# Conditioning rows kept in the heads' stage, decay rows by GpSimd's queue, and a head's tasks at fixed pieces

## The chip, the cores and the metric

The kernel runs on one core of a Trainium2 chip. A core has TensorE (PE, matmuls), VectorE (DVE), ScalarE (ACT), GpSimd (POOL) and SyncE (SP). Data come from the device's memory by DMA; SP, ACT and POOL each issue DMAs from their own instruction stream, in its order, so a DMA whose destination is not free holds up what stands behind it there. The metric is the device time of one execution in microseconds (us).

## The reference

Two layers over 256 latent and 256 context tokens of width 2048. Layer 0 is bidirectional retention with 8 heads (query and key width 256, value width 512), layer 1 windowed attention. Each layer is modulated by a projection of the conditioning vector ("ada"):

```python
c_act = silu(c); cc_act = silu(c_ctx)
mod_l = c_act @ ada_w[i] + ada_b[i]          # latent tokens; mod_c the same with cc_act
sh, sc, gt = split(mod, 3)
h = rms_norm(x, norm_gain[i]) * (1 + sc) + sh
# layer 0, per head: q, k (rope on the latent tokens), v, g = split(h @ w_in)
scores = (q @ k.T) * decay                   # gamma^(distance), one gamma for each direction and head
o = scores @ v
y = (rms_norm(o) * norm_gain * silu(g)) @ w_out
x = x + gt * y                               # and the same for the context tokens
```

## The kernel before

Numbers are fp32. An operand is split into a high part of a type that the PE takes (`wh`, `r_h`, made by ACT) and the rest (`wl`, `r_l`, made by DVE), and each product is three matmuls, L144 to L146 (`mm3`). The stages, in the order of time: up to about 137 us the inputs, layer 0's ada sums and the queries and keys of heads 0 and 1; to 235 us the q/k projections of heads 2 and 3; to 555 us the values; **555 to 1241 us the heads' stage**; to 1560 us the output projection, in a form with seven block products (M1 to M7) instead of eight, fed from `uB_d`; then the attention layer.

A **piece** is one load of 128x1024 weights (`load_w`: `wraw<-in_w` by SP, `wh` by ACT, `wl` by DVE) with the 24 matmuls that use it; `gemm_ws` runs eight pieces into four PSUM tiles `acc` and calls `hook` after each. In the heads' stage every head has a gate GEMM, and heads 4 to 7 a q/k GEMM ahead of it; heads 0 to 3 fetch q and k from DRAM (`qkr<-qk_d`). All raw blocks (weights, ada's blocks, the values) pass through one ring of five `wraw` tiles; there are three of `wh` and of `wl`.

What else is done for a head hangs on the hook, as **tasks**: `evac` (rope on q and k: ACT copies `sw`, DVE `t`, then the split), `v_load` (`wraw<-v_d` and its split), `decays` (the loads `rows<-gamT_d` and `dd<-skew_d`), `scores` (four; they read `rows` and `dd`), `output_tasks` (outputs, `ossq` sums of squares on POOL, `norm`, then `spill` and `parts`, which writes `ue` and `sg` to `uB_d`). Before, the tasks lie in one list, `pump` takes one or two of them after each piece, and what is left at a GEMM's end is run there. Beside them the hook calls `ada_step`: layer 1's and the gate's ada sums, 224 DVE instructions in all (L678, `wraw<-wraw,crow` and `ajunk<-wraw,crow`), each a block of weights times a row `crow` that is the same in all partitions; and `sums`, which prepares sums of output weights in DRAM (`wS_d`: a plain copy by ACT's queue and an accumulating DMA by POOL's, behind a tiny copy `pin_t`).

The framework's scheduler sets each engine's order from the program; `tc.issue_after(i)` keeps an instruction behind `i`. `last_lo`, `last_hi` and `last_ev` name the latest `wl`, the latest `wh` and the end of the latest `evac`.

Of the kernel before, what the change touches and what calls it, by code (L numbers as in the profile page):

```python
# [22 lines left out]
T = 512  # L23
# [29 lines left out]
def backbone(ctx: ExitStack, tc, xT_d, w0_d, wo0_d, w1_d, wo1_d, adaS_d, adaB_d,  # L53
# [68 lines left out]

    last_lo, last_hi, last_wl, last_pe, last_ev = [None], [None], [None], [None], [None]

# [213 lines left out]
    crow_d = dram.tile([2, D], F32, name="crow_d")  # L338
    adap_cm = tc.tile_pool(name="adap", bufs=1, side="right")
    adap = adap_cm.__enter__()  # L340
    pb_cm = tc.tile_pool(name="pb", bufs=1, side="right")
# [319 lines left out]

    def ada_parts(where, parts, ntk):
        for layer, kind in parts:
            part = 3 * layer + kind - 2
            asum = const.tile([P, 2, KB, ntk], F32, name="asum", tag=f"asum{ntk}")
            for q in range(2):
                pool, tags = where()
                crow = [pool.tile([P, 1024], F32, name="crow", tag=g) for g in tags[:ntk]]
                for t in range(ntk):
                    nc.sync.dma_start(out=crow[t], in_=crow_d[t, q * 1024:(q + 1) * 1024].unsqueeze(0)  # L670
                                      .to_broadcast([P, 1024]))
                yield "row"
                for kb in range(KB):
                    raw = load_raw(adaB_d[16 * part + kb, q].rearrange("p (a c) -> p a c", a=2))
                    for t in range(ntk):
                        flat = raw.rearrange("p a c -> p (a c)")
                        junk = pool.tile([P, 1024], BF16, name="ajunk", tag="ajunk") if t < ntk - 1 else flat
                        nc.vector.scalar_tensor_tensor(  # L678
                            out=junk, in0=flat, scalar=1.0, in1=crow[t],
                            op0=ALU.mult, op1=ALU.mult, accum_out=asum[:, q, kb, t:t + 1])  # L680
# [8 lines left out]
    def crows():  # L689
        return adap, ("crow0", "crow1")  # L690

    jobs = chain(ada_parts(crows, ((0, 2), (1, 0), (1, 1)), 2), ada_parts(crows, ((1, 2),), 1))
    sums = sum_jobs()

    def behind():
        return tc.issue_after(last_ev[0]) if last_ev[0] is not None else ExitStack()

    def ada_step(n=1):
        for _ in range(n):
            with tc.issue_after(last_lo[0]), behind():  # L700
                next(jobs, None)

    def ada_rest():
        for _ in jobs:
            pass

    with tc.tile_pool(name="ph", bufs=1) as ph:
# [155 lines left out]
        for _, f in later:  # L863
            f()

    pb_cm = tc.tile_pool(name="pb", bufs=1, side="right")
    pb = pb_cm.__enter__()
# [66 lines left out]
    if True:  # L934
# [11 lines left out]

        def v_load(h, i):
            raw = load_raw(v_d[h, :, 2 * i:2 * i + 2])
            for t in range(2):
                with behind():  # L950
                    split(slot_h(4 + 2 * i + t)[:, :], slot_l(4 + 2 * i + t)[:, :], raw[:, t])

        state = {"n": 0}

        def qk_evac(ps, i, base):
# [9 lines left out]
            nc.vector.tensor_tensor(out=t1, in0=t1, in1=sw, op=ALU.add)  # L965
            return split(slot_h(sl)[:, 0:L], slot_l(sl)[:, 0:L], t1)

# [3 lines left out]
        def decays(h):  # L971
            rows = pb.tile([P, 512], F32, name="rows", tag="rows", bufs=2)
            for dr in range(2):
                src = gamT_d[dr, 0:2, h, :].unsqueeze(0).to_broadcast([P, 2, P])
                nc.scalar.dma_start(out=rows[:, 256 * dr:256 * dr + 256].rearrange("p (k t) -> p k t", k=2), in_=src)
            dd = pb.tile([P, P], F32, name="dd", tag="dd", bufs=2)
            nc.scalar.dma_start(out=dd, in_=skew_d[h, 127:127 + P * 254].rearrange("(p x) -> p x", x=254)[:, 0:P])
            return rows, dd

        def scores(h, base, kb, rows, dd):  # L980
            if True:
# [9 lines left out]
                if kb >= 2:  # L991
                    d2 = pb.tile([P, L], F32, name="d2", tag="d2", bufs=2)
                    nc.vector.tensor_scalar(out=d2, in0=rows[:, L:T], scalar1=gam[:, 6 + kb - 2, h:h + 1],
                                            scalar2=None, op0=ALU.mult)
                    nc.vector.scalar_tensor_tensor(out=d2, in0=rows[:, 0:L],
# [86 lines left out]
        def evac(h, get, ks):  # L1082
            for k in ks:
                last = qk_evac(get(k), k, 0)
                last_ev[0] = last.ins if h >= 4 else None

# [5 lines left out]

        def nothing():
            pass

        def hook():
            state["n"] += 1
            n = state["n"]
# [6 lines left out]
        rate, sg = [1], None  # L1105
        rd[0] = decays(0)
        qkr = fetch(0)
        for h in range(H):
            if h < 4:
                outs = output_tasks(h - 1, sg) if h else []  # L1110
                rate[0] = 2 if h else 1
                e = [lambda g=qkr, i=i: evac(h, g, (i, 2 + i)) for i in range(2)]
                v = [lambda i=i: v_load(h, i) for i in (1, 0)]
                sc = score_tasks(h)
                if h:
                    tasks.extend([e[0], outs[0], e[1], outs[1], nothing, v[0], v[1], outs[2], sc[0], sc[1],
                                  outs[3], outs[4], sc[2], sc[3]])
                else:
                    tasks.extend([nothing, nothing, lambda e=e: (e[0](), e[1]()), lambda v=v: (v[0](), v[1]()), nothing,
                                  lambda sc=sc: (sc[0](), sc[1]()), sc[2], sc[3]])  # L1120
            else:
                tasks.extend(output_tasks(h - 1, sg))
                tasks.insert(2, nothing)
                rate[0] = 1
                accs = gemm_ws(w0_d, 3 * h, 8, h_mov, T, hook=hook)
                while tasks:
                    pump()
                evac(h, lambda k: accs[k], range(4))
                if h == H - 1:
                    break  # L1130
                tasks.extend([lambda i=i: v_load(h, i) for i in (1, 0)] + score_tasks(h))
            if h < 3:
                qkr = fetch(h + 1)
            tasks.insert(2, lambda: rd.update({h + 1: decays(h + 1)}))
            accs = gemm_ws(w0_d, 3 * h + 2, 8, h_mov, T, hook=hook)
            while tasks:
                pump()
            sg = gates(h)
            for j in range(4):
                nc.scalar.activation(sg[j // 2][:, j % 2, :], accs[j], AF.Silu)  # L1140

        sg = gates(H - 1)
        outs = output_tasks(H - 1, sg, gated=False)
        plan = ([lambda: v_load(H - 1, 1), lambda: v_load(H - 1, 0)] + score_tasks(H - 1)[:1],
                score_tasks(H - 1)[1:], outs[:1], outs[1:2] + [(M1, 2), (M1, 3)],
                [(M1, 4), (M1, 5), (M1, 6), (M4, 0), (M4, 1)], outs[2:3] + [(M4, 5), (M4, 6), (M4, 2), (M4, 3)],
                outs[3:] + [(M4, 4), (M1, 0), (M1, 1)])
# [17 lines left out]

    ada_rest()
    pb_cm.__exit__(None, None, None)
# [3 lines left out]
    with tc.tile_pool(name="pc", bufs=1, side="right") as pc:  # L1171
# [507 lines left out]
```

## Time and profile before

| | |
|---|---|
| median of 3 runs | 1986.68 us (1985.29 to 1989.74) |
| profiled execution | 1988.66 us, of which the span, first to last instruction, is 1986.9 us |
| mean granted TensorE clock | 0.993 |
| busy share of the span: PE, DVE, ACT, POOL | 97%, 75%, 41%, 19% |
| DMA traffic | 476 MB, mean 240 GB/s |

A profile row names line, engine, operation and the tiles `out<-in`. "Idle before" is the time in which the engine stood still ahead of the instruction, and the name after the arrow is what it waited for. `SPq`, `ACTq` and `POOL ... DMA_DIRECT2D` are DMA issues. Matmul durations overlap: one takes 0.39 us, but one starts every 0.227 us in the rows of a stretch without a stall.

### The profile page before, as it was taken

The numbers are of one execution on the slowest core, as the hardware profiler recorded it, in microseconds if no ns is written. First come the engines' busy times: TensorE is split into PE (matmuls) and PEld (weight loads), VectorE is DVE, ScalarE is ACT, GpSimd is POOL, SyncE is SP. The second block draws the span as 40 slices with busy tenths as digits, with TensorE's granted clock in tenths as the row PEclk, the third lists the DMA queues.
The fourth block names the chain that finished last, engine by engine and source line by source line (L and its number), as shares of the span: only waits on it lengthen the run. The fifth ranks groups of instructions, "written<-read, shape, count | busy, mean of one in ns | idle before, by whom it ended". The sixth has DMA issues, their size and how long they took to land. (4 is left out here: it accounts for less than half of the span.)

```text
span 1986.9 us, 26032 instructions
## 1 busy us (share of the span) xinstructions
PE 1925.6 (97%) x9420; PEld 1581.1 (80%) x9420; DVE 1488.7 (75%) x2250; ACT 820.6 (41%) x1218; POOL 387.2 (19%) x415
## 2 busy tenths in 40 slices
PE   8999999999989999998999999999999999999999
PEld 4678878777778778876787788888888888888887
DVE  5567687887858898777887887877779745777764
ACT  4233334334334332232232234455555434766653
POOL 1203222222212444522324031100000010000001
PEclk9999999999999999999999999999999999999999
DMA  9969788889898878878897977677777324444364
GB/s 391 410 248 303 231 238 264 265 245 294 257 283 261 266 246 256 279 237 254 241 312 220 320 278 270 209 233 260 273 235 246 109 89 159 138 139 148 127 201 149
DMA packets 144378, 476.09 MB, mean 240 GB/s; under 512 B 17625, under 2 KB 38585, under 8 KB 138617
## 3 DMA queue, kind: packets, MB, share of 16 engines
q1 hardware_dynamic: 107232, 372.64, 54.2%
q0 software_dynamic: 13360, 43.79, 11.2%
q10 hardware_dynamic: 23656, 58.00, 8.7%
q8 instruction: 74, 1.21, 0.2%
q14 instruction: 56, 0.45, 0.1%
HBM read 443.37 MB, written 99.14 MB: 273 GB/s over the span
## 5 line engine op out<-in xcount | busy, mean ns | idle before, releaser
L114 DVE TENSOR_TENSOR wl<-wraw,wh 128x1024 fp32r<-128x1024 f32 x416 | 511.5, 1235 | 272.9 <-ACT wh L136 263.3
L136 ACT CAST wh<-wraw 128x1024 fp32r<-128x1024 f32 x415 | 434.6, 1052 | 676.6 <-DMA wraw<-in_w 203.2
L144 PE MATMUL acc<-hT_h,wh 128*128 128x512 f32 x928 | 366.0, 394 | 14.5 <-DVE t L963 8.2
L146 PE MATMUL acc<-hT_h,wl 128*128 128x512 f32 x928 | 361.7, 392 | 7.2 <-DVE wl L114 7.1
L145 PE MATMUL acc<-hl,wh 128*128 128x512 f32 x928 | 363.1, 391 | 0.0
L144 PEld LDWEIGHTS acc<-hT_h,wh 128*128 128x128 f32 x928 | 175.5, 189 | 55.3 <-issue 11.4
L146 PEld LDWEIGHTS acc<-hT_h,wl 128*128 128x128 f32 x928 | 175.1, 189 | 47.2 <-DVE wl L114 10.2
L326 POOL COPY pin_t<-wl 128x1 f32<-128x1 f32 x128 | 101.2, 790 | 548.5 <-DVE wl L114 540.6
L145 PEld LDWEIGHTS acc<-hl,wh 128*128 128x128 f32 x928 | 175.5, 189 | 34.9
L678 DVE SCALAR_TENSOR_TENSOR wraw<-wraw,crow 128x1024 f32<-128x1024 f32 x128 | 165.8, 1300 | 11.8 <-DMA crow<-crow_d 8.5
L245 POOL TENSOR_TENSOR rs<-ms,mhalf 128x4 f32<-128x4 f32 (+1 forms) x23 | 32.4, 1409 | 595.1 <-DVE ms L239 294.9
L678 DVE SCALAR_TENSOR_TENSOR ajunk<-wraw,crow 128x1024 bf16<-128x1024 f32 x96 | 127.4, 1327 | 13.9 <-DMA crow<-crow_d 9.8
L146 PE MATMUL acc<-wh,hl 128*128 128x512 f32 x320 | 125.0, 391 | 0.0
L328 POOL DMA_DIRECT2D wS_d<-in_wo x128 | 101.0, 791 | 8.9 <-issue 5.9
L136 ACT CAST wh<-vt 128x1024 fp32r<-128x1024 f32 x48 | 50.5, 1053 | 100.8 <-DVE vt L117 77.1
L114 DVE TENSOR_TENSOR wl<-vt,wh 128x1024 fp32r<-128x1024 f32 x48 | 58.8, 1224 | 40.1 <-ACT wh L136 39.5
L1044 POOL TENSOR_TENSOR ue<-sg 128x512 f32<-128x512 f32 x38 | 71.5, 1888 | 74.6 <-DVE sg L1034 30.9
L144 PE MATMUL pm<-r_h 128*128 128x512 f32 (+1 forms) x216 | 76.7, 355 | 7.3 <-DVE sg L1026 6.3
L145 PE MATMUL pm<-r_l,r_h 128*128 128x512 f32 (+1 forms) x216 | 76.0, 352 | 4.3 <-DVE r_l L114 4.3
L145 PE MATMUL acc<-wl,hT_h 128*128 128x512 f32 x192 | 75.6, 394 | 1.3 <-DVE wl L114 1.3
L144 PE MATMUL acc<-wh,hT_h 128*128 128x512 f32 x192 | 74.0, 392 | 1.6 <-ACT wh L136 1.6
L146 PE MATMUL pm<-r_h,r_l 128*128 128x512 f32 (+1 forms) x216 | 75.5, 350 | 0.0
(312 smaller groups left out, 3678.0 us busy)
## 6 DMA issues: line engine op xcount, KB each, us to landing
wraw<-in_w SPq DMA_DIRECT2D x288, 512.0 KB, 5.4
wraw<-in_adaB SPq DMA_DIRECT2D x128, 512.0 KB, 5.4
wraw<-in_wo SPq DMA_DIRECT2D x80, 512.0 KB, 4.2
wS_d<-in_wo ACTq DMA_DIRECT2D x128, 256.0 KB, 5.2
wS_d<-in_wo POOLq DMA_DIRECT2D x128, 256.0 KB, 6.4
wraw<-wS_d SPq DMA_DIRECT2D x64, 512.0 KB, 4.8
araw<-in_adaS SPq DMA_DIRECT2D x28, 1024.0 KB, 11.9
wraw<-uB_d SPq DMA_DIRECT2D x20, 512.0 KB, 4.5
```

The source lines that it names most:

```text
L114: return nc.vector.tensor_tensor(out=out, in0=a, in1=hi.bitcast(F32), op=ALU.subtract)
L136: last_hi[0] = nc.scalar.copy(wh, raw).ins
L144: nc.tensor.matmul(ps, lhsT=ah, rhs=bh, start=start, stop=False, skip_group_check=skip)
L145: nc.tensor.matmul(ps, lhsT=ah, rhs=bl, start=False, stop=False, skip_group_check=skip)
L146: return nc.tensor.matmul(ps, lhsT=al, rhs=bh, start=False, stop=stop, skip_group_check=skip).ins
L245: nc.gpsimd.tensor_tensor(out=rs, in0=ms, in1=mhalf.to_broadcast([P, n]), op=ALU.pow)
L326: pin = nc.gpsimd.tensor_copy(pin_t, last_wl[0][:, 0, 0:1].bitcast(F32)).ins
L328: nc.gpsimd.dma_start(out=wS_d[i, r, q, x], in_=wo0_d[(*SUMS[i][1], r, q, x)], accum_op=ALU.add, max_dma_last_dim=4096)
L678: nc.vector.scalar_tensor_tensor(out=junk, in0=flat, scalar=1.0, in1=crow[t], op0=ALU.mult, op1=ALU.mult, accum_out=asum[:, q, kb, t:t + 1])
L1044: (nc.vector if now else nc.gpsimd).tensor_tensor(out=ue, in0=x, in1=y, op=op)
```

## The change

1. The four `crow` rows (two tokens, two halves) are loaded once at the heads' stage's start by POOL's queue and stay (three tiles of a new pool `adapB`, one of the pool `top`); before, SP loaded a pair of rows again at each half of each part, 14 loads in all.
2. `rows` and `dd` are loaded by POOL's queue, not ACT's, into one tile each instead of two, and for the head itself instead of the next one.
3. The tasks of a head stand in a list by piece. `v_load` now only issues the loads; the splits are a task of their own, `v_split`, some pieces later and behind the current `wl` and `wh`. The first instruction of `d2` waits for the current `wl` too.
4. Ada steps: up to two more after some pieces of the q/k projections of heads 2 and 3, and fixed numbers per piece in the heads' stage.
5. `sums`: every third piece, from piece 33 on two of three, instead of three of four; the rest after single stages of the output projection.
6. The last head's `uB_d<-ue` stores go by POOL's queue instead of ACT's, its value load moves to its q/k GEMM, and the preparations of M1 start earlier in its last GEMM.

Instructions by engine as ordered: PE and DVE the same number, ACT 27 fewer, POOL 31 more, SP 10 fewer.

```diff
-            for q in range(2):
-                pool, tags = where()
-                crow = [pool.tile([P, 1024], F32, name="crow", tag=g) for g in tags[:ntk]]
-                for t in range(ntk):
-                    nc.sync.dma_start(out=crow[t], in_=crow_d[t, ...].to_broadcast([P, 1024]))
+            for q in range(2):
+                if q not in rows_at:
+                    rows_at.clear()
+                    rows_at[q] = [crow(adap[0], f"crow{t}", t, q) for t in range(2)]
+        for q in range(2):          # ahead of head 0
+            rows_at[q] = [crow(adap[0], f"crow{q}{t}", t, q, nc.gpsimd) if (q, t) != (1, 1) else
+                          crow(top["pool"], "t4", t, q, nc.gpsimd) for t in range(2)]
...
-            if n <= 4 or n % 2:      # hook of the q/k projections of heads 2 and 3
-                ada_step(1 + (n <= 4))
+                ada_step(2 + (n <= 4))
...
-            rows = pb.tile([P, 512], F32, name="rows", tag="rows", bufs=2)
+            rows = pb.tile([P, 512], F32, name="rows", tag="rows")
-                nc.scalar.dma_start(out=rows[...], in_=src)
+                nc.gpsimd.dma_start(out=rows[...], in_=src)
-            dd = pb.tile([P, P], F32, name="dd", tag="dd", bufs=2)
-            nc.scalar.dma_start(out=dd, ...)
+            dd = pb.tile([P, P], F32, name="dd", tag="dd")
+            nc.gpsimd.dma_start(out=dd, ...)
...
-        def v_load(h, i):
-            raw = load_raw(v_d[h, :, 2 * i:2 * i + 2])
-            for t in range(2):
-                with behind():
-                    split(...)
+        def v_load(h):
+            for i in range(2):
+                vraw[h, i] = load_raw(v_d[h, :, 2 * i:2 * i + 2])
+        def v_split(h):
+            for i in (1, 0):
+                for t in range(2):
+                    with hold(last_lo[0], last_hi[0]):
+                        split(..., vraw[h, i][:, t])
...
-                    (nc.scalar if h == H - 1 else nc.gpsimd).dma_start(out=uB_d[m, h], in_=ue)
+                    nc.gpsimd.dma_start(out=uB_d[m, h], in_=ue)
...
         def hook():
             state["n"] += 1
-            if n % 4 != 0:
+            if state["n"] % 3 == 0 or state["n"] > 32 and state["n"] % 3 == 1:
                 next(sums, None)
-            if n > 3:
-                ada_step(2 + (n > 32 and n % 2))
-            pump(rate[0])
+            ada_step(next(state["ada"]))
+            for x in next(state["plan"]):
+                x()
...
             if h < 4:      # the lists by piece; o0, o1, norm, l0, l1 are the previous head's outputs
+                    plan = [[o0], [o1, dc], [e[0], v], [e[1], norm], [sc[0]], [l0, sc[1]], [l1, vs, sc[2]], [sc[3]]]
+                else:      # head 0
+                    plan = [[], [], [e[0]], [e[1]], [v], [sc[0]], [vs, sc[1]], [sc[2], sc[3]]]
+                begin(plan, [2 * (h > 0 or n > 3) for n in range(8)])
             else:
+                begin([[o0], [o1], [dc], [norm, v], [], [l0], [l1, vs], []], [3, 3, 3, 3, 3, 3, 2, 1])
                 accs = gemm_ws(w0_d, 3 * h, 8, h_mov, T, hook=hook)
                 evac(h, lambda k: accs[k], range(4))
+                begin([[], [], [], [sc[0]], [sc[1]], [sc[2]], [sc[3]], []], [2] * 8)
             accs = gemm_ws(w0_d, 3 * h + 2, 8, h_mov, T, hook=hook)
...
                     hook(r, kq)      # output projection
+                    if len(ms) == 1 and kq == 2:
+                        next(sums, None)
```

Three places in the orders of the engines follow. The first is SP's queue in the q/k GEMM of head 5, where one half of an ada part ends and the next begins (`in_w0` are weights, `in_adaB` ada's blocks). Before:

```order
L127 DMA wraw_8048<-in_adaB 128x1024
L670 DMA crow_7954<-crow_d_108 128x1024
L127 DMA wraw_8053<-in_adaB 128x1024
L670 DMA crow_7955<-crow_d_108 128x1024
L127 DMA wraw_8090<-in_w0 128x1024
L127 DMA wraw_8124<-in_adaB 128x1024
L127 DMA wraw_8162<-in_w0 128x1024
```

The same weights now:

```order
L134 DMA wraw_7925<-in_w0 128x1024
L134 DMA wraw_7958<-in_adaB 128x1024
L134 DMA wraw_7973<-in_w0 128x1024
L134 DMA wraw_8003<-in_adaB 128x1024
L134 DMA wraw_8008<-in_adaB 128x1024
L134 DMA wraw_8045<-in_w0 128x1024
L134 DMA wraw_8079<-in_adaB 128x1024
```

The two row loads are gone from SP's queue. The second place is ACT where the q/k GEMM of head 4 ends and its gate GEMM begins (`sw<-acc` are the evacuation's copies, `r_h<-acc` and `r_h<-t` its splits, `r_h<-wraw` the values' splits). Before:

```order
L960 COPY sw<-acc 64x256
L961 COPY sw<-acc 64x256
L120 CAST r_h<-acc 128x256
L120 CAST r_h<-t_6726 128x256
L120 CAST r_h<-acc 128x256
L120 CAST r_h<-wraw 128x512
L960 COPY sw<-acc 64x256
L961 COPY sw<-acc 64x256
L120 CAST r_h<-t_6737 128x256
L960 COPY sw<-acc 64x256
L961 COPY sw<-acc 64x256
L120 CAST r_h<-wraw 128x512
```

Now:

```order
L972 COPY sw<-acc 64x256
L973 COPY sw<-acc 64x256
L120 CAST r_h<-acc 128x256
L143 CAST wh<-wraw 128x1024
L978 CAST r_h<-t_6729 128x256
L978 CAST r_h<-t_6740 128x256
L972 COPY sw<-acc 64x256
L973 COPY sw<-acc 64x256
L120 CAST r_h<-acc 128x256
L329 DMA wS_d<-in_wo 16x4096
L972 COPY sw<-acc 64x256
L973 COPY sw<-acc 64x256
```

The values' splits are no longer among the copies, and a `wh` of the gate GEMM stands there. The third place is ACT at the end of the stage, where the last head's parts are written and the output projection's weights are split. Before:

```order
L1050 DMA uB_d<-sg 256x1x256
L136 CAST wh<-wraw 128x1024
L120 CAST r_l<-ue 128x2x256
L120 CAST bop<-ue 128x2x256
L136 CAST wh<-wraw 128x1024
L1048 DMA uB_d<-ue 128x512 x3
L136 CAST wh<-wraw 128x1024 x2
```

Now:

```order
L1064 DMA uB_d<-sg 256x1x256
L143 CAST wh<-wraw 128x1024
L120 CAST r_l<-ue 128x2x256
L120 CAST bop<-ue 128x2x256
L143 CAST wh<-wraw 128x1024 x3
L120 CAST hT_h<-wraw 128x2x256 x2
```

The three stores are no longer in ACT's queue; they stand on POOL, each behind its `ue`.

More of the change, by code (lines that the diff above doesn't have):

```diff
@@ L121, in split, with hold @@
         return sub(lo, src, hi)
-    last_lo, last_hi, last_wl, last_pe, last_ev = [None], [None], [None], [None], [None]
+    def hold(*after):
+        st = ExitStack()
+        for i in after:
+            if i is not None:
+                st.enter_context(tc.issue_after(i))
+        return st
+    last_lo, last_hi, last_wl, last_pe, last_ev = [None], [None], [None], [None], [None, None]
     def load_raw(src):
@@ L659, in backbone, with crow, ada_parts @@
     pb_cm.__exit__(None, None, None)
-    def ada_parts(where, parts, ntk):
+    rows_at = {}
+    def crow(pool, tag, t, q, queue=nc.sync):
+        c = pool.tile([P, 1024], F32, name="crow", tag=tag)
+        queue.dma_start(out=c, in_=crow_d[t, q * 1024:(q + 1) * 1024].unsqueeze(0).to_broadcast([P, 1024]))
+        return c
+    def ada_parts(parts, ntk):
         for layer, kind in parts:
@@ L666, in ada_parts @@
             for q in range(2):
-                pool, tags = where()
-                crow = [pool.tile([P, 1024], F32, name="crow", tag=g) for g in tags[:ntk]]
-                for t in range(ntk):
-                    nc.sync.dma_start(out=crow[t], in_=crow_d[t, q * 1024:(q + 1) * 1024].unsqueeze(0)
-                                      .to_broadcast([P, 1024]))
-                yield "row"
+                if q not in rows_at:
+                    rows_at.clear()
+                    rows_at[q] = [crow(adap[0], f"crow{t}", t, q) for t in range(2)]
+                    yield "row"
                 for kb in range(KB):
@@ L676, in ada_parts @@
                         flat = raw.rearrange("p a c -> p (a c)")
-                        junk = pool.tile([P, 1024], BF16, name="ajunk", tag="ajunk") if t < ntk - 1 else flat
+                        junk = adap[0].tile([P, 1024], BF16, name="ajunk", tag="ajunk") if t < ntk - 1 else flat
                         nc.vector.scalar_tensor_tensor(
-                            out=junk, in0=flat, scalar=1.0, in1=crow[t],
+                            out=junk, in0=flat, scalar=1.0, in1=rows_at[q][t],
                             op0=ALU.mult, op1=ALU.mult, accum_out=asum[:, q, kb, t:t + 1])
@@ L687, in ada_parts @@
                 yield "end"
-    def crows():
-        return adap, ("crow0", "crow1")
-    jobs = chain(ada_parts(crows, ((0, 2), (1, 0), (1, 1)), 2), ada_parts(crows, ((1, 2),), 1))
+    jobs = chain(ada_parts(((0, 2), (1, 0), (1, 1)), 2), ada_parts(((1, 2),), 1))
     sums = sum_jobs()
     def behind():
-        return tc.issue_after(last_ev[0]) if last_ev[0] is not None else ExitStack()
+        return hold(*last_ev)
     def ada_step(n=1):
         for _ in range(n):
-            with tc.issue_after(last_lo[0]), behind():
+            with hold(last_lo[0], last_ev[0]):
                 next(jobs, None)
-    def ada_rest():
-        for _ in jobs:
-            pass
     with tc.tile_pool(name="ph", bufs=1) as ph:
@@ L864, in backbone @@
             f()
+    adap_cm.__exit__(None, None, None)
+    adap_cm = tc.tile_pool(name="adapB", bufs=1, side="right")
+    adap[0] = adap_cm.__enter__()
     pb_cm = tc.tile_pool(name="pb", bufs=1, side="right")
@@ L991, in scores @@
                 if kb >= 2:
-                    d2 = pb.tile([P, L], F32, name="d2", tag="d2", bufs=2)
-                    nc.vector.tensor_scalar(out=d2, in0=rows[:, L:T], scalar1=gam[:, 6 + kb - 2, h:h + 1],
-                                            scalar2=None, op0=ALU.mult)
+                    d2 = pb.tile([P, L], F32, name="d2", tag="d2")
+                    with hold(last_lo[0]):
+                        nc.vector.tensor_scalar(out=d2, in0=rows[:, L:T], scalar1=gam[:, 6 + kb - 2, h:h + 1],
+                                                scalar2=None, op0=ALU.mult)
                     nc.vector.scalar_tensor_tensor(out=d2, in0=rows[:, 0:L],
@@ L1084, in evac @@
                 last = qk_evac(get(k), k, 0)
-                last_ev[0] = last.ins if h >= 4 else None
+                last_ev[:] = last if h >= 4 else (None, None)
         def fetch(h):
@@ L1091, in fetch, with begin @@
             return lambda k: ts[k // 2][:, k % 2]
-        def nothing():
-            pass
+        state = {"plan": None, "ada": None, "n": 0}
+        def begin(plan, ada):
+            state["plan"], state["ada"] = iter(plan), iter(ada)
         def hook():
             state["n"] += 1
-            n = state["n"]
-            if n % 4 != 0:
+            if state["n"] % 3 == 0 or state["n"] > 32 and state["n"] % 3 == 1:
                 next(sums, None)
-            if n > 3:
-                ada_step(2 + (n > 32 and n % 2))
-            pump(rate[0])
@@ L1162, in backbone @@
             dbg("uT", uT_d)
-    ada_rest()
     pb_cm.__exit__(None, None, None)
```

55 lines of the change are left out of this document (23 added, 32 removed).

## Prediction

> **What bounds the kernel now.** I read the page's busy shares first, then the stretches of the heads' stage (busy us per engine; PEclk is the granted clock).
>
> ```profile
> PE 1925.6 (97%) x9420; PEld 1581.1 (80%) x9420; DVE 1488.7 (75%) x2250; ACT 820.6 (41%) x1218; POOL 387.2 (19%) x415
> ...
> 550.00:600.00 50.00, 43.27 (x181) 34.51 (x180) 29.22 (x53) 18.18 (x33) 7.44 (x13) 0.97 0.92 286
> 600.00:850.00 250.00, 240.79 (x1130) 200.42 (x1129) 214.05 (x351) 81.82 (x139) 106.46 (x100) 0.99 0.84 261
> 850.00:950.00 100.00, 89.06 (x391) 72.06 (x390) 77.84 (x132) 27.60 (x44) 27.20 (x31) 0.95 0.80 244
> 950.00:1250.00 300.00, 290.14 (x1351) 240.30 (x1350) 244.90 (x395) 102.13 (x163) 79.28 (x78) 1.00 0.82 270
> 1250.00:1300.00 50.00, 46.32 (x254) 40.08 (x254) 38.99 (x46) 21.73 (x31) 9.87 (x3) 0.97 0.66 213
> sum 750.00, PE 709.58 PEld 587.36 DVE 605.01 ACT 251.45 POOL 230.25; mean PE 141.92 PEld 117.47 DVE 121.00 ACT 50.29 POOL 46.05
> ```
>
> TensorE bounds the kernel, and the change takes no matmul away. What it can win is TensorE's idle time where it works: 750.0 - 709.6 = 40.4 us from 550 to 1300 us. The waits of that stretch (us in total, times, longest) say for whom:
>
> ```profile
> PE acc L144 <- DVE t L963: 8.2, 5, 3.1
> PE acc L146 <- DVE wl L114: 7.1, 4, 3.9
> PE pm L144 <- DVE sg L1026: 6.3, 2, 6.0
> PE pm L1199 <- ACT wh L136: 3.6, 1, 3.6
> PE pm L253 <- POOL ossq L1030: 3.2, 2, 3.0
> ```
>
> A stall costs more than itself: behind six of them stand stretches at half the clock.
>
> ```profile
> 583.95:587.36 3.41, 3.41 (x8) 2.73 (x9) 3.41 (x7) 1.17 (x3) 1.03 (x2) 0.50 1.01 314
> 860.50:863.90 3.40, 3.40 (x8) 2.69 (x9) 3.22 (x9) 1.94 (x5) 0.00 (x0) 0.50 0.02 5
> 928.70:935.50 6.80, 3.58 (x11) 3.01 (x12) 6.80 (x10) 1.54 (x2) 0.57 (x2) 0.50 0.79 270
> ...
> sum 23.81, PE 20.59 PEld 17.03 DVE 22.72 ACT 8.87 POOL 2.44; mean PE 3.43 PEld 2.84 DVE 3.79 ACT 1.48 POOL 0.41
> ```
>
> The second begins with this stall:
>
> ```profile
> 860.43 0.74 PE L144 MATMUL acc<-hT_h,wh 128*128 128x512 f32 x1 [2.53 <-DVE t L963]
> ```
>
> Half of the 20.6 busy us in them is lost: 10.3 us, 1.7 for a stretch of 3.4. Ceiling: 40.4 + 10.3 = 50.7 us. The Trainium skill (TensorE: Matmul & The Clock Gate, "Why this matters for your kernels") lets the rate fall only after idle gaps over some 3 us. By that, the clock part of the 2.5 us stall at 860 would have another cause and stay, making the gain 1.7 smaller; the trace decides, its stretch begins with that stall.
>
> **The change, part by part.** Each gain is a group of waits, with its clock.
>
> *Start of the stage.* ACT's queue stands behind the loads of `rows`, then DVE behind their landing; SP's next weights come after the values:
>
> ```profile
> 568.60 1.05 ACT L136 CAST wh<-wraw 128x1024 fp32r<-128x1024 f32 x1 [11.11 <-DMA rows<-gamT_d]
> 571.40 0.61 DVE L993 TENSOR_SCALAR d<-rows,gam 128x256 f32<-128x256 f32 x2 [12.60 <-DMA rows<-gamT_d]
> 575.45 0.33 SPq L127 DMA_DIRECT2D wraw<-in_w  x1
> ```
>
> The `wl` waits (7.1, and 1.7 of clock: 8.8) are mostly here. Afterwards ACT issues none of these loads, `d2` stands behind `wl`, and SP has weights ahead of `qkr`. But four `crow` rows and the `rows` go in a line on POOL, and DVE reads the second half's `crow` within the first pieces. Between 0 and 8.8 I take 5: the old block goes, part of it comes back as a wait for `crow`.
>
> *`crow` resident.* 14 loads by SP become 8, of which none stands in the stage's middle:
>
> ```profile
>   DMA crow<-crow_d: 18.3, 8
> ...
> 921.98 1.22 DVE L678 SCALAR_TENSOR_TENSOR ajunk<-wraw,crow 128x1024 bf16<-128x1024 f32 x1 [6.57 <-DMA crow<-crow_d]
> 926.67 1.23 DVE L678 SCALAR_TENSOR_TENSOR wraw<-wraw,crow 128x1024 f32<-128x1024 f32 x1 [1.91 <-DMA crow<-crow_d]
> ```
>
> DVE's `sg` was late behind these, and PE waited 6.0 us: 6.3 and 1.8 of clock, 8.1. I take 8; 6 if a neighbour is late next.
>
> *Values loaded early, split late.* At a boundary ACT has the values' split between two evacuation copies:
>
> ```profile
> 858.45 0.62 ACT L120 CAST r_h<-wraw 128x512 fp32r<-128x512 f32 x1 [1.88 <-DMA wraw<-v_d]
> 859.86 0.42 DVE L963 TENSOR_TENSOR t<-acc,ropeR 128x256 f32<-128x256 f32 x1 [2.33 <-ACT sw L961]
> ```
>
> In the new order the splits are pieces away. The `t` waits are 8.2, and 1.7 of clock: 9.9. I take 8.5, with 3 as the low end, since a `wl` now stands in the evacuation.
>
> *Last head's stores on POOL.* ACT issued three stores that waited for POOL's `ue`, and the projection's `wh` behind them:
>
> ```profile
> 1252.55 8.60 POOL L1044 TENSOR_TENSOR ue<-sg 128x512 f32<-128x512 f32 x2 [17.99 <-DVE r_l L114]
> 1263.94 2.00 ACT L136 CAST wh<-wraw 128x1024 fp32r<-128x1024 f32 x2 [10.72 <-POOL ue L1044]
> ```
>
> 3.6 and 1.7 of clock: 5.3. The `wh` is free now; I take 5, 0 if SP's loads are late there.
>
> *Fixed pieces.*
>
> ```profile
> ACT sw L960 <- DMA qkr<-qk_d: 14.3, 5, 7.2
> ```
>
> The `ossq` wait (3.2 and 1.7, 4.9) came from `qkr` landing late in front of ACT's squares; with the evacuation two or three pieces into the gate GEMM, I take 4 (0 to 4.9). The rest is 40.4 - 7.1 - 6.3 - 8.2 - 3.6 - 3.2 = 12.0, and one more stretch, 13.7; these are small waits for `r_l`, `wh`, `sg` at places that the new order moves. I take half, 7 (0 to 13.7).
>
> Taken back: 5 + 8 + 8.5 + 5 + 4 + 7 = 37.5 us.
>
> What it costs:
>
> ```profile
> L114 DVE TENSOR_TENSOR wl<-wraw,wh 128x1024 fp32r<-128x1024 f32 x117 | 147.3, 1261 | 63.8 <-ACT wh L136 56.8 <-issue 6.2 <-POOL pin_t L326 0.5
> L136 ACT CAST wh<-wraw 128x1024 fp32r<-128x1024 f32 x118 | 124.1, 1052 | 342.7 <-DMA wraw<-in_w 181.2 <-PE acc L145 57.6 <-DVE wraw L678 18.3
> L678 DVE SCALAR_TENSOR_TENSOR wraw<-wraw,crow 128x1024 f32<-128x1024 f32 x114 | 148.7, 1310 | 11.8 <-DMA crow<-crow_d 8.5 <-DMA wraw<-in_adaB 2.9
> L328 POOL DMA_DIRECT2D wS_d<-in_wo x60 | 47.6, 793 | 3.7 <-issue 3.1 <-DMA wraw<-in_adaB 0.3 <-DMA crow<-crow_d 0.2
> ...
> DMA to landing us min/median/max: 2.6/5.1/11.2
> ```
>
> (All of 550 to 1300 us; the last row is the landing of `wraw`.)
>
> *Ring.* The values hold two of five `wraw` slots from load to split: 2 pieces in head 0, 4 in heads 1 to 3, 3 in heads 4 to 7, together 26. A piece then sends a block of weights and one of ada through three slots: landing L, 1.05 + 1.26 for the first, L and two of 1.31 for the second, (2L + 4.9) / 3 us a piece; a piece lasts 750 / 117 = 6.4 us. With L = 5.1 that is 5.0: hidden behind PE. The cover is gone from L = 7.2; at 9 a piece pays 1.2. I take 3 us for scattered late landings, 0 to 31.
>
> *POOL.* 28 more loads at 0.79 us are 22 us on an engine busy 230 of 750; with one `rows` tile POOL waits for the previous head's last score, pieces earlier, with `ossq`, `pin_t` and the sums behind it. ACT's 24 fewer issues free what nobody waits for. 2 us (0 to 6). Here a rule of the Trainium skill speaks against the move (DMA: Bandwidth & Descriptors, "Issuing engines are not separate DMA queues"): all issuers share the same 16 DMA engines, so another issuer saves issue time alone. By it, `rows` land no sooner and the start's 5 falls away.
>
> *Ada earlier.* Ten steps go to the q/k projections of heads 2 and 3, where DMA is full and the weights just in time:
>
> ```profile
> 148.00:164.00 16.00, 16.00 (x73) 13.23 (x72) 6.45 (x9) 3.76 (x5) 1.73 (x3) 1.00 0.94 316
> 164.00:180.00 16.00, 16.00 (x72) 13.27 (x71) 16.00 (x25) 6.60 (x8) 5.77 (x9) 1.00 1.02 324
> ```
>
> ```profile
> wraw<-in_adaB SPq DMA_DIRECT2D x128, 512.0 KB, 5.4
> ```
>
> PE has no idle time there, but DVE is busy for all 16 us of the second row. One more half-MB block ahead of the weights is 1.6 us at 320 GB/s. I take 2.5 (0 to 8). In the heads' stage ten steps of 1.3 us less: DVE is at 605 of 750, no gain of its own.
>
> *Sums.* About 18 of half a MB move to the projection, hidden under its matmuls: 0.5 (0 to 4); in the heads' stage they and the rows are some 14 MB less of about 200 (750 us at some 260 GB/s).
>
> Costs: 3 + 2 + 2.5 + 0.5 = 8. Net 37.5 - 8 = 29.5 us. The profiled execution took 1988.7 (span 1986.9 and 1.8 around it), which gives 1959.2; the median of the runs is 2.0 lower, so 1957.
>
> **Rivals.** *The ring gives half back.* If L rises to 8, a held piece costs 7.0 - 6.4 = 0.6, and 26 of them 15 us: 1972. For it speaks ACT's 181 us of waiting for weights, against it that traffic falls.
>
> *The next wait stands right behind.* The issuer doesn't matter and DMA stays as late: start, `ossq` and the rest win nothing, 8 + 8.5 + 5 - 8 = 13.5, so 1973. This is what the page's rule just named would give. For it: the DMA share of 0.92 in the stage's first 50 us; against: ACT and DVE were blocked in order there, not only by the landing.
>
> *Slower: the ring starves.* The same three slots with L at 9.5: 7.97 - 6.4 = 1.57 us in each of 26 pieces is 41 us, which eats the 29.5: 1998. It decides from L = 8.9, where 1.13 x 26 is 29.5. Landings up to 11.2 are seen, but the median is 5.1.
>
> **How the numbers follow.** The forecast (1940 to 1966) has 0.58, the ring's half 0.13, the next wait 0.12, starving 0.09, no difference 0.04, and below 1940, when nearly all of the ceiling comes, 0.04. Range 1938 to 1982: it leaves out starving, no difference and the lowest tail, and holds the two middle cases with costs a little higher. About 0.2%, 4 us, is what runs of this kernel can tell from no change: faster 0.84 (forecast, both middle cases but for a little, the tail), within it 0.06, slower 0.10.
>
> **What would show it.** Right: no `crow` wait between 600 and 1200 us, no `acc` wait for `t` over 1 us, no ACT wait for `ue` ahead of the projection, PE idle from 550 to 1300 us near 15 us, and fewer stretches at half the clock. Wrong: `wl` waits spread over pieces in which values are held, landings of `wraw` above 7 us, DVE waiting for `rows` or `crow` at the start, or PE idle at 150 to 235 us.

## The result

The changed kernel takes 1967.15 us (median of 4, 1965.91 to 1971.63) against 1986.24 us before (the table's three runs and one more): ratio 0.9905, 95% interval 0.9884 to 0.9925. A second set, beside four of the later experiments, gave 1964.63 us against 1987.90 (0.9885, 0.9865 to 0.9906). The forecast of 1957 us had the sign and the range right; of the 29.5 us that it expected, 19 to 23 came. The profiled execution took 1965.91 us, with a span of 1964.1.

The profile after, in the views of the prediction: the busy shares, the stretches of the heads' stage, and what TensorE waited for from 535 to 1290 us (us in total, times, longest).

```profile
PE 1917.0 (98%) x9420; PEld 1578.6 (80%) x9420; DVE 1493.0 (76%) x2250; ACT 817.8 (42%) x1218; POOL 401.0 (20%) x446
```

```profile
550.00:600.00 50.00, 50.00 (x228) 41.64 (x227) 35.49 (x66) 19.90 (x36) 7.99 (x13) 1.00 0.91 293
600.00:850.00 250.00, 238.45 (x1113) 197.75 (x1112) 224.90 (x363) 88.51 (x154) 104.97 (x98) 0.99 0.77 234
850.00:950.00 100.00, 98.57 (x458) 82.05 (x457) 86.01 (x140) 28.70 (x45) 32.06 (x35) 1.00 0.86 261
950.00:1250.00 300.00, 287.17 (x1344) 238.25 (x1343) 230.13 (x363) 100.53 (x157) 89.32 (x87) 0.99 0.81 258
1250.00:1300.00 50.00, 50.00 (x284) 44.05 (x283) 40.08 (x47) 23.85 (x32) 0.00 (x0) 0.98 0.68 217
sum 750.00, PE 724.19 PEld 603.73 DVE 616.61 ACT 261.49 POOL 234.34; mean PE 144.84 PEld 120.75 DVE 123.32 ACT 52.30 POOL 46.87
```

```profile
PE acc L151 <- DVE t L975: 7.6, 5, 3.2
PE pm L1212 <- ACT wh L143: 5.3, 1, 5.3
PE pm L152 <- DVE r_l L114: 5.3, 4, 1.9
PE acc L151 <- ACT sg L1154: 2.6, 3, 1.1
PE pm L151 <- DVE sg L1040: 2.0, 1, 2.0
PE pm L260 <- POOL ossq L1044: 1.2, 1, 1.2
```

TensorE's idle time from 550 to 1300 us fell from 40.4 to 750.0 - 724.2 = 25.8 us, not to the 15 that the forecast named. The stage's start (6.7 us idle, now none), the conditioning rows' stall at 932 us and most of the `ossq` wait are gone. Three groups are not: the boundary waits for `t` (8.2, now 7.6), the one at the projection's start (3.6, now 5.3) and those for `r_l` (4.3, now 5.3). A new one stands at 160 us (below). Of the stretches at a lower clock, four are left of six; they cost 7.4 us instead of 10.2 (summed from windows of 1 us).

### The profile page after: what moved, and what is told of

It is laid out like the page before. It is cut to its first block, busy times and chain, and to the rows that moved or that the text cites. A ratio compares the mean times of both kernels' runs of the same rounds, so it can differ in the third digit from the quotient of the medians.

```text
span 1964.1 us, 26030 instructions
## 1 busy us (share of the span) xinstructions
PE 1917.0 (98%) x9420; PEld 1578.6 (80%) x9420; DVE 1493.0 (76%) x2250; ACT 817.8 (42%) x1218; POOL 401.0 (20%) x446
## 4 chain that ended last, share of the span: by engine, by line
PE 73%; DVE 12%; DMA 9%; issue 3%; ACT 2%; POOL 1%; ACTq 0%; SPq 0%; DVEq 0%; POOLq 0%
PE acc L153 11%; PE acc L151 11%; PE acc L152 11%; PE acc L1212 9%; PE acc L202 6%; DMA wraw<-in_w 5%; PE acc L1209 4%; DVE wl L114 4%; PE pm L152 3%; PE pm L153 3%; PE pm L151 3%; PE acc L199 3%; PE acc L531 2%; DVE wraw L690 2%; DMA wraw<-in_adaB 2%
## 5 line engine op out<-in xcount | busy, mean ns | idle before, releaser
L333 POOL COPY pin_t<-wl 128x1 f32<-128x1 f32 x128 | 95.2, 744 | 675.9 <-DVE wl L114 666.9
L690 DVE SCALAR_TENSOR_TENSOR wraw<-wraw,crow 128x1024 f32<-128x1024 f32 x128 | 170.9, 1340 | 6.6 <-DMA wraw<-in_adaB 5.8
L690 DVE SCALAR_TENSOR_TENSOR ajunk<-wraw,crow 128x1024 bf16<-128x1024 f32 x96 | 121.9, 1270 | 6.7 <-DMA wraw<-in_adaB 6.6
L153 PE MATMUL acc<-wh,hl 128*128 128x512 f32 x320 | 125.0, 391 | 0.0
L252 POOL TENSOR_TENSOR rs<-ms,mhalf 128x4 f32<-128x4 f32 (+1 forms) x23 | 28.4, 1236 | 418.2 <-DVE ms L246 306.9
L335 POOL DMA_DIRECT2D wS_d<-in_wo x128 | 101.0, 789 | 11.1 <-issue 8.8
L151 PE MATMUL acc<-wh,hl 128*128 128x512 f32 x192 | 75.4, 393 | 0.0
L152 PE MATMUL acc<-wl,hl 128*128 128x512 f32 x192 | 74.9, 390 | 0.0
```

What stands on the lines that cost most here:

```text
L151: nc.tensor.matmul(ps, lhsT=ah, rhs=bh, start=start, stop=False, skip_group_check=skip)
L152: nc.tensor.matmul(ps, lhsT=ah, rhs=bl, start=False, stop=False, skip_group_check=skip)
L153: return nc.tensor.matmul(ps, lhsT=al, rhs=bh, start=False, stop=stop, skip_group_check=skip).ins
L333: pin = nc.gpsimd.tensor_copy(pin_t, last_wl[0][:, 0, 0:1].bitcast(F32)).ins
L335: nc.gpsimd.dma_start(out=wS_d[i, r, q, x], in_=wo0_d[(*SUMS[i][1], r, q, x)], accum_op=ALU.add, max_dma_last_dim=4096)
L690: nc.vector.scalar_tensor_tensor(out=junk, in0=flat, scalar=1.0, in1=rows_at[q][t], op0=ALU.mult, op1=ALU.mult, accum_out=asum[:, q, kb, t ...
```

## The experiments

All ratios are to the kernel before, run on the same chip; the first four ran together, then the next four, then the last four. The changed kernel was run again beside the second four only, so elsewhere a difference to it compares medians of two sets; the kernel before took 1986.2 to 1988.3 us in the four sets. The control alone ran from 1959 to 1971 us, so differences under some 4 us are not read.

**The last head's `ue` on DVE.**

```diff
-                (nc.vector if now else nc.gpsimd).tensor_tensor(out=ue, in0=x, in1=y, op=op)
+                (nc.vector if now or h == H - 1 else nc.gpsimd).tensor_tensor(out=ue, in0=x, in1=y, op=op)
```

> The changed kernel with one edit: the last head's three sums ue for M6, M7 and M3 are made by DVE instead of POOL (the stores stay on POOL's queue). Theory: the stall of 5.3 us at the projection's start is the chain POOL ue (9.62 us under a busy DVE) -> store -> release of the memory of x. Then the stall falls below 1 us, the half-clock stretch behind it goes too, and the time is 5 to 8 us under the changed kernel (about 1960). Rival: the stores' landing or the weights bound it; then the stall stays at 4 us or more and the time stays within 2 us of 1967.

1958.13 us, 0.9840 (0.9816 to 0.9864). Why it was tried is seen in the changed kernel's timeline at the projection's start, POOL, ACT and PE:

```profile
1227.18 9.62 POOL L1058 TENSOR_TENSOR ue<-sg 128x512 f32<-128x512 f32 x1 [19.63 <-DVE r_l L114]
...
1243.06 0.56 POOL L1062 DMA_DIRECT2D uB_d<-ue  x1 [0.30 <-POOL ue L1058]
```

```profile
1245.64 0.38 ACT L1217 ACTIVATE x<-acc 128x256 f32<-128x256 f32 x1 [11.14 <-DMA uB_d<-ue]
1247.01 3.58 PE L1212 MATMUL pm<-r_l,wh 128*128 128x512 f32 x7 [5.33 <-ACT wh L143]
```

The `wh` behind ACT's `x` is late, and `x` waits for the last `ue` store: the projection's `x` is put where the heads' tiles lay. The change took the stores out of ACT's queue, but the next instruction of that queue waits for the same stores through memory. With `ue` on DVE that stall is gone from the list:

```profile
PE acc L151 <- DVE t L975: 8.3, 4, 3.8
PE pm L152 <- DVE r_l L114: 3.2, 3, 1.3
```

The theory holds, and this version is faster than both kernels.

**Conditioning rows loaded again.**

```diff
+        n, debt[0] = n + debt[0], 0     # ada_step: a step that only loads rows is made up for
...
-        for q in range(2):
-            rows_at[q] = [crow(..., nc.gpsimd) ...]
+        q, = rows_at
+        rows_at[q] = [crow(adap[0], f"crow{t}", t, q) for t in range(2)]   # by SP, again at each half
```

> The changed kernel, but the conditioning rows are loaded again by SP at each half of each part, as before, two rows at a time; all else as changed. Theory: the rows' residency is worth what the prediction put on it, 8 us: DVE waits for crow again at some four to six places, 10 to 18 us in all, and the time rises by 6 to 12 us, to 1973 to 1979. Rival: the other edits moved the ada steps off the tight places, so that the waits return on DVE alone and the time rises by less than 3 us.

1976.39 us, 0.9938 (0.9915 to 0.9961): 9 us over the changed kernel. The size is the theory's; the way is not. DVE waits for `crow` 1.2 us in all. PE waits for weights (first row, from the waits; the others, timelines of SP and PE):

```profile
PE acc L151 <- ACT wh L143: 13.1, 3, 8.2
```

```profile
1040.79 0.33 SPq L134 DMA_DIRECT2D wraw<-in_w  x1
1054.47 0.33 SPq L134 DMA_DIRECT2D wraw<-in_adaB  x1
1057.92 0.33 SPq L673 DMA_DIRECT2D crow<-crow_d  x1
1058.36 0.44 SPq L134 DMA_DIRECT2D wraw<-in_adaB  x1
1059.23 0.33 SPq L134 DMA_DIRECT2D wraw<-in_w  x1
```

```profile
1067.92 0.79 PE L151 MATMUL acc<-hT_h,wh 128*128 128x512 f32 x1 [8.19 <-ACT wh L143]
```

No weights are issued from 1040.8 to 1059.2 us. The row load stands in that queue ahead of them, but its own wait there is 3.0 us; 13.7 us had passed before it, ahead of the ada block at 1054.5 us. So the rows' worth is shown as a whole, and the way it comes about isn't.

**Decay rows by ACT's queue again.**

```diff
-                nc.gpsimd.dma_start(out=rows[...], in_=src)      # and dd
+                nc.scalar.dma_start(out=rows[...], in_=src)
```

> The changed kernel, but the decay rows (rows, dd) are loaded by ACT's queue again, into the single tiles and at the changed places. Theory: the start of the heads' stage was cured because ACT's queue no longer stands behind these loads; then PE is idle 3 to 8 us again between 550 and 600 us, and with one tile each ACT also waits for the previous head's last score in later heads: 5 to 12 us slower than the changed kernel. Rival: the start was cured by the order of the loads and tasks (d2 held back, weights ahead), not by the queue: PE idle below 1 us in 550 to 600 and the time within 3 us of 1967.

1963.03 us, 0.9868 (0.9842 to 0.9893). The rival holds in the main: the start loses 1.6 us (the rival had under 1, the theory 3 to 8), and the whole loses nothing.

```profile
550.00:600.00 50.00, 48.36 (x214) 39.74 (x213) 33.40 (x60) 19.23 (x35) 6.20 (x11) 1.00 0.87 280
```

**Norm, spills and parts a piece earlier.**

```diff
-  [[o0], [o1], [dc], [norm, v], [], [l0], [l1, vs], []]
+  [[o0], [o1, dc], [norm], [v], [l0], [l1], [vs], []]
```

> The changed kernel, but in the q/k GEMMs of heads 4 to 7 the previous head's norm, spills and parts stand one piece earlier (values' load, split with them as before at pieces 4 and 7). Theory: the acc waits for t at the boundaries (7.6 us) come from POOL's ue running at the boundary and slowing DVE (wl 1.86 instead of 1.22, sw 2.41 instead of 0.42); with the parts a piece earlier ue is done by then, the t waits fall under 3 us and the time falls by 4 to 8 us. Rival: the boundary is late because the weights land late (ACT waited 2.1 us for in_w there); then the t waits stay at 6 us or more and the time within 2 us.

1975.11 us, 0.9929 (0.9906 to 0.9952), 8 us slower than the changed kernel. The `t` waits fell as the theory said, and a larger wait took their place: `norm` came before POOL's `ossq`. Its interval overlaps that of the changed kernel's first set (to 0.9925) and meets the control's at its edge (to 0.9906).

```profile
PE pm L260 <- POOL ossq L1044: 10.6, 4, 6.2
...
PE acc L151 <- DVE t L975: 1.8, 2, 1.0
```

**The changed kernel once more.**

> The changed kernel itself once more, as the control on this chip for the three that follow: 1965 to 1972 us.

1964.63 us (1959.23 to 1971.27). Its profile, of an execution of 1959 us, has the `t` waits at 4.8 us and the end stall at 5.3 again.

**Parts earlier with norm kept, and the last `ue` on DVE.**

```diff
-  [[o0], [o1], [dc], [norm, v], [], [l0], [l1, vs], []]
+  [[o0], [o1], [dc], [norm, v], [l0], [l1], [vs], []]
+  (and the last head's ue on DVE, as above)
```

> The changed kernel with the last head's ue on DVE, and in the q/k GEMMs of heads 4 to 7 the spills and parts one piece earlier while norm stays where the change put it. Theory (the boundary waits come from POOL's ue under the evacuation, and moving norm was what cost the earlier trial its time): the t waits fall to 2 us or less, the ossq wait stays at 1 to 2 us, no end stall, and the time is 12 to 16 us under the changed kernel. Rival: norm's result is not ready one piece later, PE waits for the spills' operand instead, and the time is no better than with ue on DVE alone (9 us under).

1965.42 us, 0.9889 (0.9873 to 0.9905): the rival. The end stall is gone, but `t` stays at 4.0, and PE waits 3.2 us for `rs`, norm's result on POOL. It is no faster than the control, and 7 us over the version with `ue` on DVE alone.

**And the decay rows by ACT's queue.**

> The kernel of the run before (ue of the last head on DVE, parts a piece earlier), and the decay rows by ACT's queue too. Theory: the queue of these loads is worth nothing either way: within 3 us of the run before. Rival: POOL's queue costs time, since its issues take 0.74 us each and delay ue and ossq: 3 to 6 us faster.

1957.54 us, 0.9852 (0.9833 to 0.9871), 8 us under the run before it, with intervals that just don't meet. The rival again: at these places POOL's queue costs something. Its single rows don't show where.

**POOL's sums left out** (heads 0 to 6 store one operand of each; the values are not the reference's).

```diff
+                if h < H - 1:
+                    nc.gpsimd.dma_start(out=uB_d[m, h], in_=x)
+                    continue
```

> The changed kernel with the sums ue of heads 0 to 6 left out (POOL stores one operand instead of the sum; these values are not the reference's). If POOL's ue slows DVE at the boundaries, wl and the rope steps there take 1.22 and 0.42 us again and the t waits fall from 7.6 to under 2 us; the time falls 6 to 10 us. Rival (late weights): t waits above 5 us, time within 3 us of the changed kernel.

1948.41 us, 0.9805 (0.9790 to 0.9820): 16 us under the control.

```profile
PE pm L1215 <- ACT wh L143: 5.3, 1, 5.3
...
PE acc L151 <- DVE t L975: 1.7, 2, 1.5
...
PE pm L152 <- DVE r_l L114: 0.8, 1, 0.8
```

`t` and `r_l` fall together, from 7.6 and 5.3 (4.8 and 5.4 in the control) to 1.7 and 0.8. DVE's 2250 instructions, the same as in the changed kernel, take 30 us less in all (1462.9 against 1493.0). The rope steps show it (550 to 1300 us; time in all and mean ns behind the first bar; the kernel before, the changed kernel, this one):

```profile
L964 DVE TENSOR_TENSOR sw<-sw,ropeR 128x256 f32<-128x256 f32 x32 | 13.4, 418 | 0.2 <-ACT sw L961 0.2
L976 DVE TENSOR_TENSOR sw<-sw,ropeR 128x256 f32<-128x256 f32 x32 | 18.6, 583 | 1.9 <-ACT sw L973 1.9
L976 DVE TENSOR_TENSOR sw<-sw,ropeR 128x256 f32<-128x256 f32 x32 | 13.4, 417 | 1.6 <-ACT sw L973 1.6
```

With the two steps behind it (the second `t` and the split) the three together take 43.0 us before, 51.7 now and 40.1 here: the new order has far more of POOL's sums beside them. What POOL does at a boundary is seen in the changed kernel, POOL, DVE and PE in one stretch:

```profile
840.46 1.30 POOL L1058 TENSOR_TENSOR ue<-sg 128x512 f32<-128x512 f32 x1 [5.23 <-DMA uB_d<-ue]
842.63 1.33 POOL L1058 TENSOR_TENSOR ue<-sg 128x512 f32<-128x512 f32 x1
845.36 1.58 POOL L1058 TENSOR_TENSOR ue<-sg 128x512 f32<-128x512 f32 x1
```

```profile
840.98 1.86 DVE L114 TENSOR_TENSOR wl<-wraw,wh 128x1024 fp32r<-128x1024 f32 x1 [1.88 <-ACT wh L143]
842.76 1.82 DVE L114 TENSOR_TENSOR r_l<-t,r_h 128x256 fp32r<-128x256 f32 x2
844.50 0.41 DVE L975 TENSOR_TENSOR t<-acc,ropeR 128x256 f32<-128x256 f32 x1
844.83 2.41 DVE L976 TENSOR_TENSOR sw<-sw,ropeR 128x256 f32<-128x256 f32 x1
```

```profile
845.05 0.47 PE L151 MATMUL acc<-hT_h,wh 128*128 128x512 f32 x1 [3.20 <-DVE t L975]
```

Beside each `ue` one of DVE's instructions takes 0.6 to 2.0 us longer than alone (1.22 for `wl`, 0.42 for a rope step). The first of these `ue` is late itself: it waited 5.2 us for a store, since there are two `ue` tiles. The 16 us are the worth of all that the sums do, these waits on POOL included.

**Every `ue` on DVE.**

```diff
-                (nc.vector if now else nc.gpsimd).tensor_tensor(out=ue, in0=x, in1=y, op=op)
+                nc.vector.tensor_tensor(out=ue, in0=x, in1=y, op=op)
```

> The changed kernel with every head's sums ue made by DVE instead of POOL (38 more instructions of 0.68 us on DVE, 26 us). Theory (POOL's long adds slow DVE's instructions beside them and are slowed themselves, up to 9.6 us for one): DVE's busy time rises by less than 26 us, since wl and the rope steps take their short times again; the t waits, r_l waits and the end stall shrink to 5 us together, and the time is 8 to 14 us under the changed kernel. Rival: DVE is the next bound (616 of 750 us busy); the 26 us come in bursts of five between a piece's wl and the next, PE waits for wl, and the time is within 4 us of the changed kernel or above it.

1971.44 us, 0.9924 (0.9908 to 0.9939): the rival. Taking the sums away helps; handing them to DVE makes the boundaries worse. DVE's busy time does not rise by it (1490.3 us with 38 instructions more, against 1493.0), since its others get shorter; it is the place of the sums that costs:

```profile
PE acc L151 <- DVE t L975: 18.7, 6, 5.1
```

**That, with the decay rows by ACT.**

> The run before, and the decay rows by ACT's queue. With ue gone from POOL, its queue has nothing that its DMA issues could delay: within 3 us of the run before; a gain of 4 us or more would say that the queue of these loads matters by itself.

1968.98 us, 0.9911 (0.9896 to 0.9926): the same, as the theory had it.

**The kernel before with every `ue` on DVE.**

> The kernel before with every ue on DVE, nothing else. If POOL's ue was what made the boundaries' rope step late already before the change, the t waits fall from 8.2 to under 3 us and the time falls by 6 to 12 us. If the values' splits among the copies were the cause, as the prediction had it, the t waits stay at 6 us or more.

1980.92 us, 0.9974 (0.9958 to 0.9989). The stall at the projection's start is gone; the `t` waits are 12.1 us in the profile, which is of an execution 8 us over the median. So POOL's `ue` wasn't their main cause before. In three of the six, 8.3 us together, the values' split stands ahead of ACT's copy and waits for the values; the longest:

```profile
977.30 0.62 ACT L120 CAST r_h<-wraw 128x512 fp32r<-128x512 f32 x1 [3.71 <-DMA wraw<-v_d]
978.71 0.42 DVE L963 TENSOR_TENSOR t<-acc,ropeR 128x256 f32<-128x256 f32 x1 [4.15 <-ACT sw L961]
979.28 0.76 PE L144 MATMUL acc<-hT_h,wh 128*128 128x512 f32 x1 [3.82 <-DVE t L963]
```

In the kernel before, two of the five waits, 5.7 of the 8.2 us (at 860 and 1084 us), have the same rows. So the prediction read these waits rightly. The other waits aren't settled by this run, since DVE got five more sums for each head at the same places.

**Ada steps not earlier.**

```diff
-                ada_step(2 + (n <= 4))          # q/k projections of heads 2 and 3
+                ada_step(1 + (n <= 4))
-                begin([... [sc[3]], []], [2] * 8)
+                begin([... [sc[3]], []], [3, 3, 3, 2, 2, 2, 2, 2])   # and one more in head 7
```

> The changed kernel with the ada steps of the q/k projections of heads 2 and 3 as before (ten fewer) and the ten put into the heads' stage. The stall of 2 to 4 us at 160 us goes; the heads' stage has ten more steps of 1.3 us on DVE and five more blocks in the ring. Theory (the earlier steps cost what they cost there and gain nothing later): 3 us faster. Rival (DVE is tight in the heads' stage): the stall at 160 goes and as much or more comes back later, 0 to 5 us slower.

1988.82 us, 1.0007 (0.9993 to 1.0021). The whole gain is gone. The stall at 160 us went, and several times as much came back in the heads' stage:

```profile
sum 750.00, PE 711.24 PEld 590.22 DVE 610.75 ACT 249.79 POOL 238.74; mean PE 142.25 PEld 118.04 DVE 122.15 ACT 49.96 POOL 47.75
```

```profile
PE acc L151 <- DVE t L975: 12.7, 5, 4.9
PE pm L260 <- POOL ossq L1044: 5.4, 2, 4.3
```

PE is idle 38.8 us from 550 to 1300, as long as before the change. Nine of the ten steps stand in the first pieces behind a boundary, where DVE is late already; how much of the 22 us is that place and how much the ten steps (13 us of DVE) wasn't told apart.

## Why the prediction was right or wrong

**Start of the stage: 5, measured 6.7 of idle time and its clock.** The stalls are gone. The cause given first, ACT's queue, was the lesser part: with the loads by that queue only 1.6 us come back, so the rest of the change (the order of loads and tasks) cured it. Which part of that order did it isn't shown. The Trainium skill (DMA: Bandwidth & Descriptors, "Issuing engines are not separate DMA queues") had it that another issuer saves issue time alone; the runs agree, `rows` land after 7.1 us by POOL and 6.1 by ACT. That this would leave the start's stall in place, as the prediction worked out from it, did not follow.

**`crow` resident: 8, measured 9** when it is undone. The late thing in the undone version is the weights on SP, in whose queue the row loads stand, not DVE.

**Values split late: 8.5, measured about 0.6** (3.4 in the control). This is the step that failed most, and not by its reading of the rows before. The wait that it named is mostly gone: what DVE waited for ACT's `sw` ahead of `t` (us in total from 550 to 1300 us, times, longest), before and now:

```profile
DVE t L963 <- ACT sw L961: 7.6, 7, 2.7
DVE t L975 <- ACT sw L973: 2.8, 6, 0.8
```

What failed is the overlap that it put at nothing: the new lists have the previous head's `parts` after the seventh piece of the q/k GEMM, where `pump` had them after the sixth, and at head 4 POOL's sums now run through most of the evacuation (to 846.9 us of 835.8 to 849.6), before only into its first 2.5 us (to 854.3 us of 851.8 to 863.5). DVE's steps in front of `t` get longer by it, and PE waits as long as before. The run without the sums shows that these waits are theirs (1.7). That the later piece alone brought them there isn't shown: a piece earlier `t` was 4.0 with `norm` kept and 1.8 with `norm` earlier too. No run undid the late splitting by itself.

**Last stores on POOL: 5, measured -1.7.** The second failure. ACT's queue was freed of the stores and then waited for them through the memory of `x`. The chain began with POOL's `ue`, and 8.60 us for two of them stood in the prediction's own row. Taking that away instead gave 9 us.

**`ossq`: 4, measured 2.0** of idle time; **the rest: 7**, of which `wh` at the boundaries (3.3, now 0.2) came, and `r_l` (4.3, now 5.3) did not; it falls to 0.8 without POOL's sums. These two groups were not undone by a run of their own.

**Costs.** *Ada earlier*, 2.5, measured 3.2 us of idle time at its place:

```profile
160.48 0.50 PE L151 MATMUL acc<-hT_h,wh 128*128 128x512 f32 x1 [2.67 <-ACT wh L143]
161.74 0.50 PE L153 MATMUL acc<-hT_h,wl 128*128 128x512 f32 x1 [0.52 <-DVE wl L114]
```

But "no gain of its own" was wrong: DVE at 605 of 750 us is an average, and at the boundaries it has no room. *The ring*, 3: `wl` waits in the stage are 0.6 us, `wraw` lands after a median of 5.0; this rival and its slower sister did not come. *Sums*, 0.5: TensorE is full while DMA's share rises to 0.94.

```profile
1400.00:1450.00 50.00, 50.00 (x287) 43.87 (x287) 39.32 (x58) 26.33 (x39) 2.89 (x6) 1.00 0.94 307
```

*POOL*, 2: where POOL's `ue` is in place, the two kernels with ACT's queue took 4 and 8 us less than their likes with POOL's; only the second difference is clear of the scatter, and by it the 2 was too small.

The stage gave less than forecast, and part of the time came from places that the sum doesn't name, which is luck. TensorE's idle time in the values' stage (240 to 555 us), where the change only has the ada steps run ten ahead, fell from 7.5 to 4.0 us; why isn't shown. A stretch at half the clock at 24 us, 1.7 us and ahead of everything that was changed, stands in the profile before and not in the one after; it is there again in the version with the last `ue` on DVE. Of the 22.8 us between the two spans the stage gave 14.6 of idle time and 2.8 of clock, the values' stage 3.5, the stretch at 24 us 1.7, the place at 160 us took 3.2, and some 3 us aren't placed.

So the forecast came out a quarter to a half too large because two groups, 13.5 of the 37.5 us, brought nothing: in both the named wait went, and another took its place. Of the signs that it gave, no `crow` wait and fewer slow stretches came; a `t` wait of 3.2 us, ACT's 11.1 us for a store of `ue` and 25.8 us of idle time instead of 15 speak against it, and so do the 3.2 us at 160 us. The rival with this mechanism ("the next wait stands right behind") had it at the other places: it let the start, `ossq` and the rest win nothing, and kept the 8.5 and the 5. There it came out the wrong way round. Its 1973 lies about as near to the measured 1965 to 1967 as the forecast's 1957, so the number doesn't decide between them; the waits do.

## What to carry to other kernels

Before a wait is booked as a gain, look at what the new order puts in the same place, on the other engines too, and ask what else the waiting instruction needs: the next operand in its queue, and the memory that its result is put into, which may be released only by the store that was just moved elsewhere. An engine at 80% on the average can be the bound at a few places; there instructions moved in can cost more than their duration (ten steps of 1.3 us, some 22 us). Two engines that share a path must be read side by side: durations that grow in one engine's rows are the sign.

## What was not expected of the hardware

A sum of 128x512 on POOL took 9.62 us while DVE had no gap (7 instructions in a row until 1235.6 us), and 1.25 to 1.31 us once DVE stood still:

```profile
1227.62 2.35 DVE L114 TENSOR_TENSOR wl<-wraw,wh 128x1024 fp32r<-128x1024 f32 x2
1229.89 3.49 DVE L117 TENSOR_TENSOR wraw<-wraw 128x1024 f32<-128x1024 f32 x3
1233.30 2.35 DVE L114 TENSOR_TENSOR wl<-wraw,wh 128x1024 fp32r<-128x1024 f32 x2
```

The Trainium skill (SBUF — State Buffer, "SBUF: two separate sides") calls the ports that DVE and GpSimd share an exclusive lock: a DVE instruction with two inputs in SBUF and a GpSimd instruction that reads SBUF exclude each other, and whichever starts first holds it for the whole instruction. The rows agree that one waits for the other, in both directions: the sum above ends 1.2 us after DVE's last instruction, and DVE's 0.42 us step took 2.41 beside a `ue`. They agree on the operands too: `t<-acc,ropeR`, one operand of which is in PSUM, takes 0.42 us on the average before, after and without the sums, where `sw<-sw,ropeR` goes from 0.42 to 0.58 and back. Who started first isn't borne out by them: the step of 2.41 us starts 0.5 us ahead of the `ue` and ends 0.3 us behind it.

Half the clock did not follow every stall: after the one of 3.20 us at 845 us the next 3.4 us were granted 0.59, after that of 2.05 us at 1115.8 us 1.00, while before the change 2.53 us at 860 had been enough.

```profile
845.20:848.60 3.40, 3.40 (x10) 2.68 (x11) 2.92 (x4) 0.96 (x3) 3.03 (x5) 0.59 0.73 161
1115.80:1119.30 3.50, 3.46 (x18) 2.99 (x19) 3.50 (x6) 0.00 (x0) 2.22 (x2) 1.00 1.04 380
```
